# A hybrid two-layer backbone on one core: the RWKV stage, its group norms and the Hyena filters put in a recorded order, and late conditioning moved to VectorE

## The chip, the cores and the metric

The kernel runs on one core of a Trainium2 chip. A core has a matrix engine (TensorE, PE), three engines for element-wise work (VectorE or DVE, ScalarE or ACT, GpSimd or POOL) and SyncE (SP), which here issues every DMA. Each engine works through its own instructions in order; semaphores order the engines among each other. The metric is the device time of one execution in microseconds (us), lower is better.

## What is computed

Two layers over 1024 latent tokens of width 1024, with 256 context tokens in front. Each layer: `n = rmsnorm(h) * (1 + scale) + shift`, a token mixer with output `y`, then `h = h + gate * y`. Shift, scale and gate are `silu(c) @ ada_w[i] + ada_b[i]`, for the vector `c` of the latents and for `c_ctx` of the context; this is the conditioning. Layer 0 mixes with retention and RWKV-7 side by side, layer 1 with a Hyena long convolution (by FFT, with filters from a small network) and a neighbourhood attention. All is float32; large products are made of three matmuls of rounded high and low parts. RWKV, per head of 64 and in both directions, is a recurrence:

```
def step(s, inp):
    r_t, w_t, k_t, v_t, kk_t, a_t = inp
    sa = einsum('bhvk,bhk->bhv', s, -kk_t)
    s = s * w_t + sa * (kk_t * a_t) + v_t * k_t      # outer products
    return s, einsum('bhvk,bhk->bhv', s, r_t)
...
gn = (rw_y - mean) * rsqrt(var + eps) * rw_ln_w + rw_ln_b
rw_o = (gn + bonus) * silu(u_gate)
```

## The kernel before

Tokens lie in 10 blocks of 128. The program runs in stages.

- **Stage A** (`phase_a`): the first layer's shift and scale (`ada_quarter`), the norms, and the dense projections. `Dense.cols` and `Shift.tile` multiply all tokens with 512 weight columns at a time, 24 matmuls for a PSUM tile (`dnp`, `mmps`), four PSUM buffers; `wtiles` loads weights (`wraw`) and splits them on ACT (`whi`) and POOL (`wlo`). Retention runs among it.
- **Stage B** (`phase_b`): RWKV in 10 groups `g` of 128 tokens per direction `d`, a group as two steps `t` of 64 tokens; 16 matrices of 64x64 (8 heads, two steps) per group and direction. `stage1` calls `half` for each direction and pair of head pairs (40 half-groups in all): `lora` makes decay and rate, ACT, DVE and POOL make the operands `AR` and `BK`, PE turns `BK` into `BT` (`btp`). Then PE makes scores `sc`, which DVE masks into `Ga` and `Gr`. `lora` has one PSUM buffer, `sc` and `btp` share two (`b1`).
- `inverse` inverts the unit-triangular 64x64 matrices: it stores `Ga` to DRAM, loads its diagonal 32-blocks as `AL`, 128 lanes of them, solves 31 steps of two DVE operations (`tm`, `RR`, L956 and L958), stores and loads back into `TT`. `merge` fills the off-diagonal 32-block with three products of 32x32x32 (`t11p`, `xp`, `t21p`, L979).
- `recur` carries the state, 20 times in sequence: `rp` (L993 with the state, L996 with `Ga`), copy to `RH`, `up` with `TT`, copy to `UV`, `sp` (L1008), state update `S`, `SP`; results `Yg` by `rp` with `Gr` (L1016). `RwkvOut.block` applies group norm and gate to a block once both directions have it.
- In the same stage run the rest of the conditioning (`ada_gate`, `ada_cols`: blocks of 128 columns, weight-stationary on two columns of `c`, `adaps` L327, `adat` L293) and, after the last `stage1`, the Hyena filters (`hyena_kernels`).
- **Stage C and later**: output projection of layer 0 (`ops` on `chi`), layer 1's dense projections, attention, convolution, output. None of it is touched by the change, but that the filters' last matmuls run among the first `ops`.

In what order an engine takes its instructions is decided when the program is built: a scheduler of the language simulates the program and takes the ready instruction of highest priority. `Rwkv.step` gives the RWKV work a higher priority than the rest, and the generators `side` and `blocks` lay conditioning and group norms between the steps.

## Time and profile before

| what | us |
|---|---|
| three runs, median (lowest, highest) | 2404.95 (2404.92, 2412.53) |
| the profiled execution, its own time | 2408.1 |
| its span | 2406.3 |
| PE busy | 2206.3 (92%) |
| DVE, ACT, POOL busy | 1213.9, 930.2, 791.6 |

The profile is of one execution. Busy time of PE counts a matmul from its start to its modelled end, so matmuls that follow each other overlap in it. A float32 matmul is two passes, and so two records. The granted clock is the share of TensorE's full 2.4 GHz that it was given; its other level is half of that. In the row of tenths for 40 slices of the span, PE stands at 6 to 9, and its clock falls below 9 tenths in slices 12 to 21, which are the RWKV stage, and in slice 33.

### The profile page before, as it was taken

To read this page: it belongs to the slowest core of one execution; us is meant where nothing else is said; L and a number is where in the kernel's file an instruction comes from. 1 tells how busy PE (TensorE), PEld (TensorE's weight loads), DVE (VectorE), ACT (ScalarE), POOL (GpSimd) and SP (SyncE) were. 2 spreads that over 40 slices of the span, in tenths; PEclk is the share of its full clock that TensorE was granted. 3 is DMA by queue.
4 is the path that set the end of the run, shared out by engine and by line. 5 is a ranking of instruction groups with operands and counts; after the bars stand their busy time and mean duration, and the time that the engine had idled before them with its cause. 6 is when DMAs were issued, how large, how long until landed. Compare 5 with 4: busy or idle time off the path is not lost. (4 is left out here: it accounts for less than half of the span.)

```text
span 2406.3 us, 44212 instructions
## 1 busy us (share of the span) xinstructions
PE 2206.3 (92%) x16800; PEld 1854.7 (77%) x16800; DVE 1213.9 (50%) x3043; ACT 930.2 (39%) x1996; POOL 791.6 (33%) x1040
## 2 busy tenths in 40 slices
PE   7999999999989788898868899999979999989997
PEld 3778878777856677777766689889968888878987
DVE  6301222234347687777777756610036666634438
ACT  4321124445345354444335543321124444444432
POOL 2313625453556243333214534521111011010133
PEclk9999999999988787788889999999989999999999
DMA  7323333544276544455455443433276462175453
GB/s 245 95 78 106 116 115 123 155 126 136 91 211 180 119 124 126 108 134 138 101 145 170 151 160 107 148 115 109 75 184 162 130 169 93 53 242 156 132 161 123
DMA packets 398365, 325.66 MB, mean 135 GB/s; under 512 B 135038, under 2 KB 337928, under 8 KB 397898
## 3 DMA queue, kind: packets, MB, share of 16 engines
q1 hardware_dynamic: 398154, 322.85, 46.5%
q8 instruction: 133, 2.18, 0.4%
q14 instruction: 78, 0.64, 0.1%
HBM read 227.58 MB, written 95.17 MB: 134 GB/s over the span
## 5 line engine op out<-in xcount | busy, mean ns | idle before, releaser
L386 POOL TENSOR_TENSOR wlo<-wraw,whi 128x512 fp32r<-128x512 f32 (+1 forms) x60 | 81.6, 1380 | 354.7 <-ACT whi L385 303.0
L418 PE MATMUL dps<-n1hi,whi 128*128 128x512 f32 x448 | 187.5, 418 | 0.1
L418 PE MATMUL dps<-n1hi,wlo 128*128 128x512 f32 x448 | 177.4, 396 | 0.0
L418 PE MATMUL dps<-n1lo,whi 128*128 128x512 f32 x448 | 177.1, 395 | 0.0
L418 PE MATMUL dnp<-wlo,nhi 128*128 128x512 f32 x400 | 159.1, 399 | 2.9 <-POOL wlo L402 2.9
L418 PE MATMUL dnp<-whi,nlo 128*128 128x512 f32 x400 | 158.3, 397 | 0.0
L418 PE MATMUL dnp<-whi,nhi 128*128 128x512 f32 x400 | 153.3, 399 | 1.6 <-ACT whi L401 1.6
L402 POOL TENSOR_TENSOR wlo<-wraw,whi 128x512 fp32r<-128x512 f32 (+1 forms) x72 | 92.3, 1291 | 131.4 <-ACT whi L401 126.5
L418 PE MATMUL mmps<-nhi,whi 128*128 128x512 f32 (+1 forms) x336 | 123.4, 368 | 2.9 <-ACT vto L533 2.1
L327 PE MATMUL adaps<-aw,sc 128*2 128x128 f32 (+1 forms) x640 | 114.2, 335 | 11.6 <-DMA aw<-in_ada_w 9.6
L418 PE MATMUL mmps<-nlo,whi 128*128 128x512 f32 (+1 forms) x336 | 120.8, 361 | 0.0
L418 PE MATMUL mmps<-nhi,wlo 128*128 128x512 f32 (+1 forms) x336 | 119.6, 365 | 0.0
L956 DVE TENSOR_TENSOR tm<-RR,AL 128x126 f32<-128x126 f32 (+22 forms) x310 | 99.7, 322 | 19.5 <-DMA AL<-la 13.3
L1254 POOL TENSOR_TENSOR hn<-hn,xr 128x256 f32<-128x256 f32 x60 | 47.2, 791 | 175.4 <-DVE hn L1253 158.8
L418 PEld LDWEIGHTS dps<-n1hi,wlo 128*128 128x128 f32 x448 | 85.1, 190 | 18.6
L327 PEld LDWEIGHTS adaps<-aw,sc 128*2 128x2 f32 x640 | 55.3, 94 | 56.4 <-issue 16.7
L958 DVE TENSOR_TENSOR RR<-RR,tm 128x126 f32<-128x126 f32 (+22 forms) x310 | 94.6, 305 | 6.2
L418 PE MATMUL ops<-whi,clo 128*128 128x256 f32 x320 | 89.7, 287 | 6.1 <-DVE clo L1187 6.1
L418 PEld LDWEIGHTS dps<-n1hi,whi 128*128 128x128 f32 x448 | 85.9, 192 | 11.0 <-ACT whi L385 0.6
L418 PEld LDWEIGHTS dps<-n1lo,whi 128*128 128x128 f32 x448 | 85.6, 191 | 10.5
L418 PE MATMUL ops<-whi,chi 128*128 128x256 f32 x320 | 92.8, 292 | 0.0
L418 PEld LDWEIGHTS dnp<-wlo,nhi 128*128 128x128 f32 x400 | 75.7, 189 | 22.0 <-POOL wlo L402 4.7
(400 smaller groups left out, 6188.9 us busy)
## 6 DMA issues: line engine op xcount, KB each, us to landing
aw<-in_ada_w SPq DMA_DIRECT2D x32, 512.0 KB
kkr<-kkr SPq DMA_DIRECT2D x40, 384.0 KB
wraw<-in_odd_w_in SPq DMA_DIRECT2D x56, 256.0 KB
wraw<-in_even_w_in SPq DMA_DIRECT2D x48, 256.0 KB
bi<-in_nab SPq DMA_DIRECT2D x64, 192.0 KB
aw<-in_ada_w SPq DMA_DIRECT2D x8, 1024.0 KB
spec<-KS SPq DMA_DIRECT2D x32, 256.0 KB
h<-hn SPq DMA_DIRECT2D x16, 512.0 KB
```

Of the source, the lines that this page charges most:

```text
L327: nc.tensor.matmul(ps[0:2, :n], self.sc[:, k, :], w[:, k, :], start=k == 0, stop=k == 7)
L386: (lo_eng or nc.gpsimd).tensor_tensor(lo[:, kk:kk + 4], raw, hi[:, kk:kk + 4].bitcast(F32), op=ALU.subtract)
L402: nc.gpsimd.tensor_tensor(lo[:, :n], raw[:, :n], hi[:, :n].bitcast(F32), op=ALU.subtract)
L418: nc.tensor.matmul(ps, a, b, start=start and n == 0, stop=stop and n == 3 * nk - 1)
L956: nc.vector.tensor_tensor(t3, RR[:, 0:n, q:q + 1].to_broadcast([P, n, w]), AL[:, q:q + 1, q + 1:32].to_broadcast([P, n, w]), op=ALU.mult)
L958: nc.vector.tensor_tensor(RR[:, 0:n, q + 1:32], RR[:, 0:n, q + 1:32], t3, op=ALU.add)
L1254: add.tensor_tensor(h[:, cs], h[:, cs], x[:, cs], op=ALU.add)
```

## The change

What it does, in the order of the program:

- `ada_block`: the vector `c` is padded to 32 columns (`scw`), and the eight products of a block go to four column groups of 32; the four partial sums are added by the small matmul with `sel` that turns them.
- Conditioning that ran in stage B (both gates, layer 1's shift and scale) runs in stage A (`ada_late`): DVE adds up weight tiles of 128x512 times `c`, 16 operations a block of 512 columns, 8 blocks; PE sums over the partitions once a block. `Dense.cols` and `Shift.tile` advance it by one tile after each of their PSUM tiles.
- Stage B is written as generators which say what engine they need, for how long, and what they wait for; `Sched` plays them through when the program is built, with fixed durations, and the five engines keep that order.
- `lora` makes both directions at once, matmuls of the two row halves in turn; it takes two `b1` buffers, which it now shares with `sc` and `btp`.
- One eviction masks a whole `sc` tile into `G`, which replaces `Ga` and `Gr`.
- `inverse` works on 16-blocks: 15 steps of two operations, on POOL. `merge` makes the full inverse from the block-diagonal one by four rounds of 64x64x64 products (`mg`) with a DVE eviction after each; a round goes in two halves of eight matrices.
- In `recur` matmuls with a zero half use 64 rows instead of 128, and `sp` takes its two output halves in turn.
- Filters end within stage B's order; their operands have two buffers where they had one, and `psh` two PSUM buffers.

```
+class Sched:
+    HOP, LOOK = 0.12, 0.15
+    ...
+    def run(self):
+        while True:
+            ...
+            first = {}
+            for _, e, _, at, *_ in self.ready:
+                first[e] = min(first.get(e, 1e9), max(self.free.get(e, 0.0), at))
+            e = min(first, key=first.get)
+            r = min((r for r in self.ready if r[1] == e and r[3] <= first[e] + self.LOOK * (e != "")), key=lambda r: r[0])
+            ...
+    def ada_late(self, pool, psp):
+        ...
+        for layer, c0 in [(0, 2048 + 512 * j) for j in range(2)] + [(1, 512 * j) for j in range(6)]:
+            acc = [pool.tile([P, 512], F32, name="acc", tag=f"acc{j}", bufs=2) for j in range(2)]
+            for k in range(8):
+                w = pool.tile([P, 512], F32, name="aw", tag="aw", bufs=3)
+                nc.sync.dma_start(w, self.i["ada_w"][layer, k * P:(k + 1) * P, c0:c0 + 512])
+                for j in range(2):
+                    c = self.sc[:, k, j:j + 1]
+                    if k:
+                        nc.vector.scalar_tensor_tensor(acc[j], w, c, acc[j], op0=ALU.mult, op1=ALU.add)
+                    else:
+                        nc.vector.tensor_scalar(acc[j], w, c, None, op0=ALU.mult)
+                yield
...
         for k in range(8):
-            nc.tensor.matmul(ps[0:2, :n], self.sc[:, k, :], w[:, k, :], start=k == 0, stop=k == 7)
-        return ps[0:2, :n]
+            g = 32 * (k % 4)
+            nc.tensor.matmul(ps[g:g + 32, :n], self.sc[:, k, :], w[:, k, :], start=k < 4, stop=k > 3)
+        return ps[:, :n]
...
+    def lora(self, g, hp):
+        ...
+        pss = [self.b1([P, 2, 2, P], "lora") for _ in range(2)]
+        for j, w in enumerate((self.w2, self.a2)):
+            for q, d in itertools.product(range(2), range(2)):
+                p = 2 * hp + q
+                nc.tensor.matmul(pss[d][:, j, q, :], w[HALF[d], p * P:(p + 1) * P], wa[HALF[d], j, :], start=True, stop=True)
...
+    def inverse(self, g):
+        ...
+        yield "get", "al"
+        ...
+        nc.sync.dma_start(AL, self.blocks("la", g))
+        t += 4.5
+        for q in range(15):
+            t = yield "POOL", 0.63, t
+            ...
+            nc.gpsimd.tensor_tensor(t3, RR[:, 0:n, q:q + 1].to_broadcast([P, n, w]),
+                                    AL[:, q:q + 1, q + 1:16].to_broadcast([P, n, w]), op=ALU.mult)
+            nc.gpsimd.tensor_tensor(RR[:, 0:n, q + 1:16], RR[:, 0:n, q + 1:16], t3, op=ALU.add)
...
+    def merge(self, g):
+        ...
+        for j in range(4):
+            for hp in range(2):
+                ...
+                ps = self.pc.tile([P, 8, C], F32, name="mg", tag="mg", bufs=1)
+                for u in range(8):
+                    for d in range(2):
+                        ...
+                        nc.tensor.matmul(ps[HALF[d], u, :], lh, rh, start=True, stop=True)
...
-            for h, p, d in each:
-                nc.tensor.matmul(sp[HALF[h], p, d, :], R["bt"][d, p // 2][:, (p % 2) * NS + t, h * C:h * C + C], uh(d, t, p, h),
+            for p, d, h in itertools.product(range(4), range(2), range(2)):
+                nc.tensor.matmul(sp[HALF[h], p, d, :], half("bt", d, p)[:, (p % 2) * NS + t, h * C:h * C + C], uh(d, p, h),
                                  start=True, stop=True)
...
+        E = mybir.EngineType
+        with tc.manual_schedule(engines={E.PE, E.DVE, E.Activation, E.Pool, E.SP}):
+            sch.run()
```

How instructions stand at three places, before and after. On PE, where a group's inverse is completed among other groups' scores; before:

```order
L979 MATMUL xp<-TX,Ga 32x32 x32
L921 MATMUL sc<-AR,BK 128x128 x8
L857 MATMUL lora<-wa,a_6097 128x128 x2
L327 MATMUL adaps<-aw,sc 2x128 x8
L979 MATMUL t21p<-TT_6116,TY 32x32 x32
L891 MATMUL btp<-cst,BK 128x128 x4
```

At the same work after (`mg` is the PSUM tile of `merge`, `HTt` the off-diagonal factor):

```order
L1239 MATMUL mg<-lt,G 64x64 x16
L989 MATMUL lora<-wa,w_6448 128x128 x4
L989 MATMUL lora<-wa,a_6449 128x128 x4
L1239 MATMUL mg<-lt,G 64x64 x16
L1239 MATMUL mg<-ld,HTt 64x64 x16
L1120 MATMUL sc<-AR,BK 128x128 x4
L1239 MATMUL mg<-ld,HTt 64x64 x16
```

The conditioning (`adaps`) is gone from between them, and the merge stands in runs of 16 instead of 32.

On DVE in the RWKV stage, where a group's substitution runs; before:

```order
L958 TENSOR_TENSOR RR<-RR,tm 128x7x18
L865 SCALAR_TENSOR_TENSOR cum<-scm,tw 128x256
L981 COPY TX<-t11p 32x512
L923 TENSOR_TENSOR Ga<-sc,cst 128x256
L925 TENSOR_TENSOR Gr<-sc,cst 128x256
L956 TENSOR_TENSOR tm<-RR,AL 128x136
L290 COPY adarow<-adaps 2x128
```

After, the same engine with the recurrence's copies (`RH`, `UV`) and the merge's evictions (`HTt`):

```order
L1287 COPY RH<-rp_8719 64x512
L1122 TENSOR_TENSOR G<-sc,cst 128x2x2x128
L1298 COPY UV<-up 64x512
L1050 SCALAR_TENSOR_TENSOR AR<-kkr,Pt_6461 128x4x64
L1122 TENSOR_TENSOR G<-sc,cst 128x2x2x128
L1309 TENSOR_TENSOR S<-S,sp 128x512
L1311 TENSOR_TENSOR S<-S,PCt 128x512
L1038 SCALAR_TENSOR_TENSOR cum<-scm,tw 128x256
L1083 SCALAR_TENSOR_TENSOR tw<-tw,kkr 128x256
L1244 TENSOR_TENSOR HTt<-mg,cst 128x512
```

And POOL after, which had none of the substitution before; `km`, `AR`, `BK` and `PCt` are the operands of the next half-group:

```order
L1196 TENSOR_TENSOR tm<-RR,AL 128x28
L1198 TENSOR_TENSOR RR<-RR,tm 128x14x2
L1196 TENSOR_TENSOR tm<-RR,AL 128x15
L1198 TENSOR_TENSOR RR<-RR,tm 128x15
L1085 TENSOR_TENSOR km<-km,kkr 128x256
L1053 TENSOR_TENSOR AR<-kkr,Pt_6460 128x4x64
L1090 TENSOR_TENSOR BK<-tw,Pi 128x4x64
```

The substitution has moved from among DVE's evictions to a closed run on POOL, ahead of the operands of later groups.

On DVE in stage A, at the first gate and the first query and key block; before:

```order
L649 SCALAR_TENSOR_TENSOR gt<-th,dnp 128x512 x10
L615 TENSOR_TENSOR rqk<-dnp,rope 128x512
L616 TENSOR_TENSOR rb<-dnp,rope 128x512
L615 TENSOR_TENSOR rqk<-dnp,rope 128x512
L616 TENSOR_TENSOR rb<-dnp,rope 128x512
```

After, with the late conditioning's sums (`acc`) between the evictions of the dense tiles (`dnp`):

```order
L385 SCALAR_TENSOR_TENSOR acc<-aw,scw,acc 128x512 x14
L750 SCALAR_TENSOR_TENSOR gt<-th,dnp 128x512 x8
L387 TENSOR_SCALAR acc<-aw,scw 128x512
L396 TENSOR_TENSOR adab<-adaps,adab 2x512
L387 TENSOR_SCALAR acc<-aw,scw 128x512
L385 SCALAR_TENSOR_TENSOR acc<-aw,scw,acc 128x512 x7
L750 SCALAR_TENSOR_TENSOR gt<-th,dnp 128x512
L385 SCALAR_TENSOR_TENSOR acc<-aw,scw,acc 128x512 x7
```

The sums stand in runs of up to 14 in front of evictions.

## Rows read from the trace of the kernel before

**Rows 1.** Stretches: length; busy us (count) of PE, PEld, DVE, ACT, POOL; clock; DMA.

```profile
58.50:672.90 614.40, 595.76 (x3028) 469.26 (x3027) 161.56 (x320) 216.25 (x391) 270.72 (x394) 0.99 0.38 114
...
1200.00:1393.80 193.80, 156.53 (x1593) 127.03 (x1593) 142.18 (x326) 93.13 (x193) 77.87 (x87) 0.91 0.48 149
...
672.90:1434.00 761.10, 651.87 (x7502) 539.58 (x7501) 548.43 (x1434) 345.48 (x774) 302.53 (x436) 0.85 0.53 144
692.80:1195.50 502.70, 436.25 (x5479) 364.60 (x5478) 376.70 (x1046) 224.88 (x539) 204.06 (x333) 0.82 0.54 135
```

**Rows 2.** Tiles: passes, ns min/median/max of one, first and last start.

```profile
L418 PE MATMUL mmps<-nhi,wlo x336: 276/394/629, 381.3 to 672.9; 128*128 128x512 f32 x112, 128*128 128x256 f32 x56
...
L857 PE MATMUL lora<-wa,w x160: 272/273/581, 692.8 to 1144.6; 64*128 64x128 f32 x160
...
L921 PE MATMUL sc<-AR,BK x640: 271/272/580, 707.9 to 1195.5; 64*128 64x128 f32 x160
...
L418 PE MATMUL ops<-whi,chi x320: 274/281/682, 1393.8 to 1540.0; 128*128 128x256 f32 x160
```

**Rows 3.** PE groups, 672.9 to 1434: passes | busy us, mean ns | idle before, releaser.

```profile
L921 PE MATMUL sc<-AR,BK 64*128 64x128 f32 x640 | 87.0, 307 | 4.9 <-DVE Gr L925 3.9 <-DVE tm L956 0.8
L327 PE MATMUL adaps<-aw,sc 128*2 128x128 f32 x512 | 81.5, 316 | 2.5 <-DVE adarow L341 1.2 <-DVE mc L295 0.8 <-DMA aw<-in_ada_w 0.5
...
L1008 PE MATMUL sp<-UV,BT 128*64 128x64 f32 x640 | 43.6, 243 | 5.2 <-DVE UV L1005 5.1
...
L857 PE MATMUL lora<-wa,w 64*128 64x128 f32 x160 | 34.9, 348 | 1.2 <-ACT tw L861 1.0
L857 PE MATMUL lora<-wa,a 64*128 64x128 f32 x160 | 34.8, 348 | 11.6 <-ACT tw L861 11.6
...
L1388 PE MATMUL d2ps<-d2r,f 128*128 128x512 f32 x47 | 27.5, 668 | 2.6 <-ACT S L1368 1.1 <-ACT d2r L1381 1.1 <-ACT KS L1347 0.4
L996 PE MATMUL rp<-UV,Ga 128*64 128x64 f32 x640 | 25.8, 229 | 0.0
...
L979 PE MATMUL t21p<-TT,TY 32*32 32x32 f32 x640 | 16.3, 218 | 8.8 <-DVE TY L981 8.6
L979 PE MATMUL t11p<-cst,TT 128*32 128x32 f32 x640 | 15.8, 210 | 8.1 <-DMA TT<-lt 8.1
L979 PE MATMUL xp<-TX,Ga 32*32 32x32 f32 x640 | 15.6, 213 | 5.1 <-DVE TX L981 5.1
...
L293 PE MATMUL adat<-cst,adarow 2*128 2x2 f32 x32 | 7.1, 288 | 11.5 <-DVE adarow L290 11.5
...
L418 PE MATMUL mmps<-nlo,whi 128*128 128x256 f32 x1 | 0.3, 281 | 0.0
```

**Rows 4.** PE in order of time: start, us, instruction.

```profile
715.85 0.27 PE L857 MATMUL lora<-wa,a 64*128 64x128 f32 x1
715.86 0.27 PE L921 MATMUL sc<-AR,BK 64*128 64x128 f32 x1
715.96 0.27 PE L857 MATMUL lora<-wa,a 64*128 64x128 f32 x1
```

**Rows 5.** DVE groups, 672.9 to 1434, columns as in rows 3.

```profile
L956 DVE TENSOR_TENSOR tm<-RR,AL 128x126 f32<-128x126 f32 (+22 forms) x310 | 99.7, 322 | 19.5 <-DMA AL<-la 13.3
L958 DVE TENSOR_TENSOR RR<-RR,tm 128x126 f32<-128x126 f32 (+22 forms) x310 | 94.6, 305 | 6.2
...
L1327 DVE TENSOR_TENSOR HK<-hkps,win 128x512 f32<-128x512 f32 x32 | 22.0, 686 | 11.6 <-PE hkps L1325 6.7 <-POOL EO L1332 4.7
...
L1094 DVE TENSOR_TENSOR fa<-fa,fv 128x512 f32<-128x512 f32 x10 | 8.4, 841 | 3.3 <-POOL fa L1093 3.2
```

**Rows 6.** POOL groups around the RWKV stage, columns as in rows 3.

```profile
L888 POOL COPY PCt<-Pt 128x4 f32<-128x4 f32 x40 | 9.9, 259 | 5.7 <-ACT Pt L870 3.4 <-DVE S L1011 1.4 <-DVE tm L956 0.9
...
L734 POOL TENSOR_TENSOR st<-SS,gch 64x128 f32<-64x128 f32 x18 | 8.3, 458 | 1.3
```

**Rows 7.** PE in order of time, start of the program, one conditioning product.

```profile
50.97 3.61 PE L327 MATMUL adaps<-aw,sc 128*2 128x256 f32 x16
```

More of the change, by code (lines that the diff above doesn't have):

```diff
@@ new lines, in __init__, with start @@
+        self.T = {}
+    def start(self):
+        add, ALL = self.sch.add, range(self.NG)
+        for g in ALL:
+            add(2 + g / 100, self.wa(g))
+            for hp in range(2):
+                add(2 + g / 100 + hp / 1000, self.lora(g, hp))
+            for n in range(4 * g, 4 * g + 4):
+                r = 2 + g / 100 + n % 4 / 2000
+                for f in (self.load, self.chain, self.keys, self.scores, self.turn, self.end):
+                    add(r, f(n))
+            for t in range(self.NS):
+                add(1.5, self.values(g, t))
+            add(1 + g / 100, self.inverse(g))
+            add(0.5, self.merge(g))
+        add(0, self.recur())
@@ L862, in half, with chain @@
-        th, ta = tw[:, 0], tw[:, 1]
+        return [nat(L[:, :, j, :]) for j in range(3)], v4, u4
+    def chain(self, n):
+        nc, sch, T, pf, C = self.s.nc, self.sch, self.T, self.pf, self.C
+        g, d, hp = self.split(n)
+        ca, cr = (0, 64) if d == 0 else (64, 0)
+        yield "wait", ("tw", n), ("kkr", n)
+        yield "get", "tmp"
+        (kt, kkt, rt), v4, u4 = self.views(n)
+        th = T["tw", n][:, 0]
+        t = yield "ACT", 0.43
+        sch.mark(("tmp", n), t)
         nc.scalar.activation(th, th, AF.Copy, scale=0.5, bias=0.5)
-        cum = pf.tile([P, 2, P], F32, name="cum", tag="cum", bufs=1)
+        yield "DVE", 0.87
+        cum = pf.tile([P, 2, P], F32, name="cum", tag="cum", bufs=2)
@@ L983, in recur, with end @@
-    def recur(self, g, R):
-        s, D, pl, pc, C, NS = self.s, self.D, self.pl, self.pc, self.C, self.NS
-        nc, S, SP, RH = s.nc, self.S, self.SP, self.RH
-        uh = lambda d, t, p, h: R["uv"][d, t][:, p, h * C:h * C + C]
-        each = [(h, p, d) for h in range(2) for p in range(4) for d in range(2)]
-        copy = (nc.vector.tensor_copy, nc.scalar.copy)
-        for t in range(NS):
+        sch.put("b1", t)
+        sch.mark(("bt", n), t)
+    def end(self, n):
+        t = yield "wait", ("used", n), ("ar", n)
+        self.sch.put("kkr", t)
+        t = yield "wait", ("prod", n), ("G", n), ("bt", n), ("pc", n)
+        self.sch.put("tmp", t)
+        if n % 2:
+            yield "wait", ("used", n - 1)
+            self.sch.put("tw", t)
@@ L1013, in recur @@
             for h in range(2):
+                yield "ACT", 0.62
                 nc.scalar.copy(SP[HALF[h], :, :, h, :], S[HALF[h]])
[L1015 to L1024 removed]
@@ L1146, in phase_b, with after_scores, over @@
-    return hy, right, f1
-def phase_c(s, D, hy, right, keep):
+        sf = ExitStack()
+        pf, pb, ph = pool(sf, "b_f", side="right"), pool(sf, "b_ps", space=PSUM), pool(st, "b_h")
+        rw = Rwkv(s, D, sch, pl, pc, pf, pb)
+        f1 = []
+        def after_scores():
+            sf.close()
+            f1.append(pool(keep, "f1", side="right").tile([P, 8, 2, 2, 64], F32, name="f1"))
+            return f1[0], pool(right, "b_k", side="right"), pool(right, "b_kp", space=PSUM)
+        def over():
+            n = 4 * rw.NG - 4
+            t = yield ("wait", *((k, n + j) for j in range(4) for k in ("prod", "G", "bt", "pc")))
+            sch.mark("over", t)
@@ L1173, in phase_c @@
              for c in range(4)]
-        for _ in hy:
-            pass
         n1 = None
@@ L1207, in phase_c @@
             if not n1:
-                right.close()
                 pn = pool(keep, "n1", side="right")
```

987 lines of the change are left out of this document (640 added, 347 removed).

## The prediction

> **What bounds the kernel now.** I read the stretches first, then the first and last starts of the tiles that mark stages, then the TensorE (PE) groups of the middle stage, then single matmuls, then VectorE (DVE) and GpSimd (POOL).
>
> [rows 1] cut the span where its character changes. In the dense stage A (58.5 to 672.9 us) PE is busy 595.8 of 614.4 us, 97%, at a granted clock of 0.99: only less PE work helps there. In the middle, stage B, from the last dense matmul at 672.9 us to 1434.0 us, PE is busy 651.9 of 761.1 us, 86%, at a mean clock of 0.85, so part of it at 1.2 GHz; DVE is busy 548.4, ScalarE (ACT) 345.5, POOL 302.5. No engine is full. 110 of the core's idle PE microseconds lie here, and this is the stage that the change rewrites.
>
> [rows 2] give the marks: dense matmuls start until 672.9, `lora` opens stage B at 692.8, the last score matmul starts at 1195.5, the first output projection (`ops` on `chi`) at 1393.8. A few filter matmuls run among the projections until 1434, which is why I close the stage there; what follows is untouched, and I count it as before.
>
> **The change, part by part.** PE groups overlap at their edges: the 34 groups of the stretch, from 87.0 to 0.3 us [rows 3], sum to 754.3 us against a union of 651.9, so a group counts 0.864 of its own busy time.
>
> 1. Conditioning leaves stage B. `adaps` is 81.5 us and `adat` 7.1 us [rows 3], 88.6 together: 88.6 x 0.864 = 77 us less on PE.
>
> 2. `lora` alternates the two row halves. Now all passes of a `lora` use the same 64 rows, 34.9 + 34.8 us [rows 3]. Where a `lora` and an `sc` pass on different halves meet, two start within 0.01 us and the next 0.11 us later [rows 4], so two go at once. Half of 69.7 x 0.864 is 30 us less; if the pairs don't form, 0.
>
> 3. The state product `sp` alternates its output halves. It costs 43.6 us for 320 matmuls, 136 ns each; `rp` on `Ga`, of the same size but with halves alternating, 25.8 us, 81 ns each [rows 3]. 17.8 x 0.864 = 15 us less.
>
> 4. The inverse works on 16-blocks and is completed by 1280 matmuls of 64x64x64 instead of 960 of 32x32x32. The three old groups cost 16.3 + 15.8 + 15.6 = 47.7 us [rows 3]. No 64x64x64 pair exists in the trace. Nearest: the 81 ns above, 103 us in all, 55.5 x 0.864 = 48 us more. Low end: the 49 ns of an `xp` (15.6 / 320), 13 us more. High end: 136 ns, 109 us more. I take 48, since that row has the same columns and alternation.
>
> 5. DVE loses the 620 substitution steps, 99.7 + 94.6 = 194.3 us [rows 5]. It gains 80 merge evictions of 128x512, 0.686 us each as `HK` [rows 5], 55 us against 21 us for the old copies at the same price. The masks stay alike (80 evictions for 160 of half the size). All in all DVE comes to some 385 us.
>
> 6. POOL gains 300 steps of at most 64 elements. Between the 259 ns of a four-element copy and the 458 ns of a 64-element product [rows 6] they cost 78 to 137 us; with 107 and without the memsets of UV, POOL ends near 385 us. Half of these steps wait for the step before, and behind the stage's own POOL work: that latency is a rival below. ACT loses copies and stays near 335.
>
> 7. PE work left in the stretch: 651.9 - 77 - 30 - 15 + 48 = 578 us. It is still the fullest engine by far, so the time is this divided by how full PE can be kept. Two rows bound it: 86%, today's stage B, and 97%, the dense stage, which hardly waits. I take the middle, 91.3%: for more, because DVE goes from 72% of the stretch to about 60%, and its substitution steps no longer stand between an eviction and the matmul that waits for it; for no more, because the chain of the recurrence stays, and filling with conditioning in the first 100 us is gone. 578 / 0.913 = 633 us, 128 less than 761. If the order recorded in advance misjudges a wait, everything behind it on that engine waits too, SyncE's (SP) DMA issues included; 86% would still give 672, 89 less.
>
> 8. Stage A takes the conditioning. 128 DVE operations of 128x512, at most 0.841 us each as `fa` [rows 5], are 108 us, put on a DVE that is busy 161.6 of 614.4 us [rows 1]. They hide behind PE as long as evictions wait less than the four PSUM buffers allow. On PE come 8 matmuls of 512 columns, 1.15 us each by `d2ps` (27.5 us for the stretch's 24 [rows 3]), and 32 of one column, at most 7.1 / 16 = 0.44 each: 9 to 23 us, and stage A has no idle time to hide them. I take 12. The 64 loads of 256 KB move the same bytes as the 32 taken out of B; they pass SP ahead of weight loads in A, which have a spare buffer. At the start eight conditioning products of 3.6 us each [rows 7] are spread over four column groups; most of it waits for loads, so 5 us less (0 to 8). Together 7 us more.
>
> 9. The tail. The filters no longer mix with the output projections: their last two transforms run alone on PE, with evictions between. I count that within the 91.3%.
>
> Sum: -128 + 7 = -121 us on an execution of 2408.1 us (span 2406.3): 2287. The median of the runs shown, 2405.0, lies 3 us lower: **2284 us**.
>
> **A rule beside the rows.** Two of the old merge products, `xp` and `t21p`, alternate row groups within one PSUM bank, and `xp`, on 32 rows, costs 15.6 us where `t11p`, on all rows, costs 15.8 [rows 3]: no sign of a wait, though passes of 32 columns may be too short to show one. The Trainium skill, TensorEngine Tiling (Array Packing), Restrictions and Gotchas, says that different row tiles cannot access the same PSUM bank at the same time. By that rule the new merges, whose two row halves write one bank, would go one by one; the time is the second rival's.
>
> **The rivals.**
>
> *Denser than that.* With 49 ns merges (543 us of PE work) and PE at 97%, stage B takes 560 us: -201 + 7, 2211 us. For it: PE would be the only full engine, and a denser PE holds the higher clock, as 0.99 in stage A shows. Against it: [rows 1], where even the last part before the projections, mostly filters, keeps PE at 81%.
>
> *Merges one by one.* 136 ns each put 61 us more on PE: 639 / 0.913 = 700, -61 + 7, 2351 us. For it: `sp`, with its halves not alternating, shows that price. Against it: `xp`.
>
> *The freed time isn't used.* Work leaves PE and DVE, but the recurrence and the DMA round trips of the inverse set the pace, and PE idles instead. PE at 78% gives 741 us: -20 + 7, 2392 us. For it: 81% in the last stretch of [rows 1] at a DVE that is not full either. Against it: the substitution, the longest part of that round trip, halves its steps.
>
> *Slower: two PSUM buffers become the bound.* Before, `lora` has a buffer of its own beside the two of `sc` and `btp`; after, all three share two, and one `lora` takes both until ACT has read them. Per half-group that is four holds (two `sc`, one `btp`, one of `lora`) on two buffers. Today the 40 half-groups take 502.7 us [rows 1], 12.6 each, so it decides from 6.3 us a hold. A hold needs 1.09 us of matmuls (87.0 / 80) and 0.69 of eviction, 1.8 us; queued behind other work on DVE and ACT it could reach 7 us: 14 x 40 = 560, 57 more, +7: 2469 us. Against it: that needs over 4 us of queueing at every hold.
>
> **How the numbers follow.** Forecast 0.47 (its own range 2245 to 2325), denser 0.20, merges one by one 0.13, not used 0.13, slower 0.07. The range runs from 2200, below the densest case, to 2375, above the merge case and the better part of the unused one; left out are the rest of that case and the slower one, under 0.2. A difference of 0.3% (7 us) is about what a measurement of this kernel can tell from none. Forecast, denser, merges and most of the unused case lie more than that below 2405: faster 0.90; a little of the unused case: same 0.03; slower 0.07.
>
> **What would show it.** The last dense matmul starts 5 to 20 us later than 672.9 and `ops` on `chi` first near 1290. PE groups after: no `adaps` past the dense stage, `lora` near 35 us, `sp` near 26, the merges (`mg`) near 103; 62 or 174 would speak for the bounds. PE in stage B should be busy about 91% of some 630 us; below 80% the unused case is right. A dense stage longer by over 25 us would mean that the DVE bursts or the extra loads hold up its evictions. I would be wrong altogether if `lora` waits for buffers more than it does now, or if stage B is not shorter.

## The result and the profile after

The changed kernel takes 2379.6 us (median of four runs, 2369.9 to 2385.6) against 2408.7 us before (four runs, 2404.9 to 2420.4): a ratio of 0.988, 95% interval 0.9847 to 0.9913. The forecast was 2284 us, the range 2200 to 2375. The sign was right, a quarter of the gain came (29 us of 121), and the time lies 5 us outside the range. The profiled execution after took 2369.9 us, span 2368.1; it is the fastest of the four, and the account by stages below is of this one.

The same four cuts serve both kernels: the last dense matmul (`mmps`), the first and the last state product (`sp`), and the last matmul of the first output projection (`ops`). I call the stretch from the last dense matmul to the first `sp` the lead-in, and that from the first to the last `sp` the recurrence. Tiles of after (passes, ns of one, first and last start); those of before are [rows 2]:

```profile
L514 PE MATMUL mmps<-nhi,wlo x336: 276/393/632, 410.7 to 714.9; 128*128 128x512 f32 x112, 128*128 128x256 f32 x56
...
L989 PE MATMUL lora<-wa,w x160: 272/373/579, 760.4 to 1135.5; 64*128 64x128 f32 x160
...
L514 PE MATMUL ops<-whi,chi x320: 274/281/684, 1380.3 to 1511.7; 128*128 128x256 f32 x160
```

Stretches of before between these cuts, after its dense stage [rows 1] (length; busy us and count of PE, PEld, DVE, ACT, POOL; clock; DMA share; GB/s):

```profile
672.90:817.90 145.00, 128.71 (x1015) 93.98 (x1014) 97.74 (x250) 74.99 (x190) 73.19 (x113) 0.80 0.70 185
817.90:1294.50 476.60, 399.66 (x5748) 348.01 (x5747) 358.88 (x1005) 197.51 (x446) 159.80 (x251) 0.83 0.49 125
1294.50:1540.20 245.70, 223.66 (x1574) 195.66 (x1571) 160.85 (x361) 108.61 (x198) 115.90 (x106) 0.98 0.46 148
1540.20:2406.30 866.10, 812.48 (x5219) 724.92 (x5217) 399.01 (x1004) 308.21 (x731) 157.52 (x162) 0.98 0.47 137
```

The same of after, with the dense stage as the first row:

```profile
52.60:714.90 662.30, 630.45 (x3142) 487.08 (x3140) 274.89 (x467) 217.74 (x395) 284.00 (x396) 0.97 0.44 131
714.90:860.30 145.40, 96.09 (x763) 76.63 (x761) 51.53 (x92) 61.98 (x159) 74.65 (x141) 0.61 0.50 124
860.30:1254.90 394.60, 345.90 (x6068) 309.39 (x6070) 261.51 (x468) 193.21 (x455) 232.57 (x457) 0.94 0.65 146
1254.90:1512.00 257.10, 221.87 (x1580) 194.20 (x1576) 153.10 (x352) 106.36 (x196) 114.63 (x102) 0.98 0.43 138
1512.00:2368.10 856.10, 806.40 (x5219) 719.79 (x5217) 397.12 (x1004) 308.71 (x731) 157.55 (x162) 0.98 0.48 139
```

So the account is: start -6, dense stage +48, lead-in 0, recurrence -82, filters and first projection +11, the rest -10; together the 38 us between the two spans. Most of the gain is in the recurrence, and the dense stage gives more than half of it back. The rest has the same code in both kernels; in the runs below that stretch takes 855 to 866 us, so its 10 us are scatter.

TensorE groups of after from 714.9 to 1420 us (passes | busy us, mean ns | idle before, releaser), and the conditioning's two groups in the dense stage; [rows 3] are those of before, and one more of before stands last:

```profile
L1239 PE MATMUL mg<-TT,HTt 64*64 64x64 f32 x1280 | 49.2, 230 | 8.7 <-DVE TT L1248 8.7
L1239 PE MATMUL mg<-lt,G 64*64 64x64 f32 x640 | 27.0, 235 | 4.4 <-DMA lt<-lt 3.4 <-DVE HTt L1244 0.9
L1302 PE MATMUL sp<-UV,BT 128*64 128x64 f32 x640 | 25.5, 239 | 10.4 <-DVE UV L1298 10.4
L1239 PE MATMUL mg<-ld,HTt 64*64 64x64 f32 x640 | 23.8, 226 | 2.7 <-DVE HTt L1244 1.7 <-DVE TT L1248 1.0
L989 PE MATMUL lora<-wa,w 64*128 64x128 f32 x160 | 22.3, 366 | 21.1 <-DMA wa<-wa 16.3 <-ACT tw L998 2.4 <-DVE G L1122 2.4
L989 PE MATMUL lora<-wa,a 64*128 64x128 f32 x160 | 17.3, 320 | 0.0
...
L1120 PE MATMUL sc<-AR,BK 64*128 64x128 f32 x640 | 106.7, 320 | 22.0 <-POOL BK L1092 14.1 <-DVE G L1122 2.3 <-ACT BT L1146 2.0
...
L1324 PE MATMUL rp<-UV,G 128*64 128x64 f32 x640 | 23.6, 231 | 0.0
```

```profile
L395 PE MATMUL adaps<-acc,one 128*2 128x512 f32 x16 | 9.2, 704 | 0.5 <-ACT vto L633 0.5
L403 PE MATMUL adaps<-one,acc 128*128 128x1 f32 x64 | 7.9, 244 | 0.0
```

```profile
L1016 PE MATMUL rp<-UV,Gr 128*64 128x64 f32 x640 | 52.9, 246 | 3.6 <-ACT UV L1005 3.6
```

The prices of the parts that the forecast named are close to it: merges 100.0 us, `sp` 25.5, `lora` 39.6 as the sum of its two groups. (These two now overlap; together they keep TensorE busy 33.9 us, where the 69.7 us of before did not overlap.) What the parts were worth is not close.

### The profile page after: what moved, and what is told of

The parts are those of the page before. It is cut to its first block, busy times and chain, and to the rows that moved or that the text cites. A ratio compares the mean times of both kernels' runs of the same rounds, so it can differ in the third digit from the quotient of the medians.

```text
span 2368.1 us, 44174 instructions
## 1 busy us (share of the span) xinstructions
PE 2130.7 (90%) x16976; PEld 1807.1 (76%) x16976; DVE 1172.1 (49%) x2487; ACT 912.2 (39%) x1976; POOL 875.7 (37%) x1271
## 5 line engine op out<-in xcount | busy, mean ns | idle before, releaser
L514 PE MATMUL dnp<-whi,nhi 128*128 128x512 f32 x400 | 160.1, 411 | 1.4 <-ACT whi L497 1.3
L1120 PE MATMUL sc<-AR,BK 64*128 64x128 f32 x640 | 106.7, 320 | 22.0 <-POOL BK L1092 14.1
L514 PE MATMUL mmps<-nhi,wlo 128*128 128x512 f32 (+1 forms) x336 | 121.1, 368 | 0.1
L1120 PEld LDWEIGHTS sc<-AR,BK 64*128 64x128 f32 x640 | 90.6, 219 | 32.7 <-POOL BK L1092 15.1
L385 DVE SCALAR_TENSOR_TENSOR acc<-aw,scw,acc 128x512 f32<-128x512 f32 x112 | 96.8, 915 | 22.0 <-DMA aw<-in_ada_w 21.6
L497 ACT ACTIVATE whi<-wraw 128x512 fp32r<-128x512 f32 (+1 forms) x72 | 43.0, 605 | 135.7 <-DMA wraw<-in_even_w_in 91.6
L514 PEld LDWEIGHTS dnp<-whi,nhi 128*128 128x128 f32 x400 | 76.3, 192 | 21.4 <-ACT whi L497 4.0
```

The lines of the kernel that those rows point to most:

```text
L385: nc.vector.scalar_tensor_tensor(acc[j], w, c, acc[j], op0=ALU.mult, op1=ALU.add)
L497: nc.scalar.activation(hi[:, :n], raw[:, :n], AF.Copy)
L514: nc.tensor.matmul(ps, a, b, start=start and n == 0, stop=stop and n == 3 * nk - 1)
L1120: nc.tensor.matmul(ps[:, u, :], T["bk", n][HALF[h], u, :], T["ar", n][HALF[h], u, :], start=True, stop=True)
```

## The experiments

Each row is a profiled execution cut as above, with the median of the timed runs and their ratio to runs of before that were timed beside them (medians 2407 to 2411 us).

| kernel | dense stage | lead-in: to `lora` + on | recurrence | DVE busy in it | median us | ratio (95%) |
|---|---|---|---|---|---|---|
| before | 614.4 | 19.9 + 125.1 | 476.6 | 358.9 | 2408.7 | 1 |
| after | 662.3 | 45.5 + 99.9 | 394.6 | 261.5 | 2379.6 | 0.988 (0.9847-0.9913) |
| a1 | 640.6 | 54.5 + 100.4 | 400.5 | 261.4 | 2370.5 | 0.9836 (0.9816-0.9856) |
| a2 | 655.3 | 45.8 + 99.9 | 405.5 | 259.1 | 2375.5 | 0.9864 (0.984-0.9888) |
| a3 | 653.8 | 46.2 + 100.2 | 400.4 | 262.2 | 2376.6 | 0.9866 (0.9845-0.9887) |
| a4 | 615.2 | 54.4 + 110.8 | 451.5 | 327.9 | 2406.9 | 0.9985 (0.997-0.9999) |
| a5 | 662.4 | 18.2 + 121.1 | 423.7 | 264.5 | 2402.6 | 0.9971 (0.9953-0.999) |
| a6 | 646.8 | 16.8 + 99.8 | 401.5 | 261.7 | 2340.7 | 0.971 (0.967-0.975) |
| a7 | 614.9 | 54.4 + 113.6 | 410.0 | 271.6 | 2365.5 | 0.9801 (0.977-0.9831) |
| a8 | 636.2 | 16.8 + 114.1 | 418.8 | 271.7 | 2355.9 | 0.9793 (0.9755-0.9832) |
| a9 | 661.4 | 45.8 + 108.9 | 407.0 | 261.8 | 2393.8 | 0.9941 (0.9918-0.9965) |
| a10 | 662.6 | 46.5 + 99.7 | 402.5 | 261.3 | 2385.1 | 0.9921 (0.989-0.9952) |
| a11 | 666.1 | 46.0 + 121.8 | 503.0 | 258.2 | 2502.0 | 1.0409 (1.0367-1.0451) |
| b1 | 618.2 | 13.6 + 158.2 | 480.4 | 359.4 | 2436.1 | 1.0093 (1.0058-1.0129) |
| b2 | 617.9 | 13.8 + 129.7 | 481.9 | 359.4 | 2417.3 | 1.0035 (1.0016-1.0055) |
| c1 | 663.8 | 46.4 + 100.7 | 463.9 | 321.4 | 2443.7 | 1.0141 (1.0121-1.016) |
| c2 | 666.8 | 17.9 + 143.6 | 487.9 | 277.1 | 2457.7 | 1.0208 (1.0187-1.0229) |
| c3 | 638.5 | 21.0 + 114.0 | 447.2 | 279.3 | 2383.5 | 0.99 (0.9883-0.9918) |
| c4 | 637.7 | 22.8 + 115.3 | 415.3 | 270.4 | 2362.2 | 0.9804 (0.9772-0.9836) |
| c5 | 657.4 | 46.6 + 99.4 | 404.9 | 260.5 | 2384.5 | 0.9912 (0.9878-0.9947) |

Where the RWKV stage is the changed kernel's own (after, a1 to a3, a6), its recurrence reads 394.6 to 405.5 us: that is the scatter against which a difference in that column has to stand, and against before the gain is 71 to 82 us. Where the dense stage is the changed kernel's own (after, a5, a9 to a11, c1, c2, c5), it reads 657.4 to 666.8 us. The expectations count the recurrence and its first step from the first `rp`, which in after starts 6.5 us ahead of the first `sp` (853.8 against 860.3 us).

### What the conditioning costs the dense stage (a1 to a3)

a1 does the loads and VectorE steps for the first of eight row blocks only, a2 all loads, a3 all VectorE steps on one load:

```
 for k in range(8):
+    if k: yield; continue                     # a1
     w = pool.tile(...); nc.sync.dma_start(w, ...)   # a3: only if k == 0
     for j in range(2):                              # a2: multiply only if k == 0
```

> The changed kernel with only the first of the eight row blocks of each conditioning block loaded and multiplied (8 loads and 16 VectorE operations in place of 64 and 128; the conditioning matmuls stay, so the modulation values and gates are wrong). From the first dense matmul to the last the changed kernel takes 662 us against 614 before. Theory 'conditioning holds up the dense stage': most of the 48 us go with this, only the conditioning's own 17 us of TensorE stay, so about 632 us here and about 2350 us in all (ratio to before near 0.975). Rival 'the dense stage grew for another reason' (the retention's share of it, the lower clock at its start, buffers): the stretch stays above 650 us and the time above 2370.

> The changed kernel with all 64 conditioning loads, but only the first row block of each conditioning block multiplied on VectorE (16 operations in place of 128). If the loads, which pass SyncE ahead of weight loads, cost the dense stage its time, it stays near 662 us and the whole near 2378. If VectorE's operations do it, by standing in front of evictions and weight preparation, it comes down to about 632 us and 2350 in all, as with the first row block only.

> The changed kernel with all 128 conditioning operations on VectorE, but each conditioning block loads only its first row block and uses it eight times (8 loads in place of 64). If VectorE's operations themselves cost the dense stage its time: near 662 us there, 2378 in all. If it is the loads, or VectorE standing still until a load lands with evictions queued behind it (21.6 us of such waits in the trace of after): about 632 us and 2350.

Without the late conditioning the dense stage takes 614.9 us (a7). With its matmuls and an eighth of the rest it takes 640.6, with the other loads added 655.3, with the other VectorE steps added instead 653.8, with both 662.3. No single part is to blame: the matmuls with that eighth bring 26 us, the other loads alone 15, the other steps alone 13, both together 22. (a2 and a3 lie only 2 to 4 us below the scatter of the full stage.) Neither forecast of a2 and a3 came, 632 or 662, and a1 stayed 9 us above its 632 and 20 above its 2350.

By [rows 1] and the rows above, 35 of the 48 us are busy time of TensorE (630.5 against 595.8), 17 of them the conditioning's own matmuls, and 13 are waits (31.9 us against 18.6). The other 18 us of busy time come with a granted clock of 0.97 in place of 0.99; no run takes them apart. The longest waits of after's dense stage (waited for: us, times, longest):

```profile
PE hyps L1791 <- DMA hw<-in_hw: 6.9, 1, 6.9
PE gtp L758 <- DVE gt L750: 6.5, 2, 3.3
PE dnp L514 <- POOL wlo L498: 4.3, 7, 1.4
```

The first, for a load of the filter network's weights, is not among before's waits of this stage; the others are there in smaller size.

The whole gained less than the stage in each case: in a1 the stage is 21.7 us shorter and the first `sp` comes 12 us sooner, because `lora` then starts 54.5 us behind the dense stage and not 45.5. Something else held it, which a5 and a6 ask.

### What holds the RWKV stage back (a5, a6)

SyncE's queue in after, between the last dense matmul and the first `lora` (start, us, line, transfer):

```profile
741.45 0.33 SPq L879 DMA_DIRECT2D cat<-rn  x1
741.83 0.43 SPq L872 DMA_DIRECT2D rG<-rz  x1
749.35 0.32 SPq L879 DMA_DIRECT2D cat<-rn  x1
749.71 0.43 SPq L929 DMA_DIRECT2D eye<-in_eyel  x1
750.19 1.76 SPq L1167 DMA_DIRECT2D UV<-vt  x3
752.06 1.00 SPq L935 DMA_DIRECT2D ld<-Z  x2
753.10 2.10 SPq L935 DMA_DIRECT2D lt<-Z  x2
755.24 1.27 SPq L1167 DMA_DIRECT2D UV<-vt  x1
756.56 1.34 SPq L970 DMA_DIRECT2D wa<-wa  x1
```

The retention of the dense stage still works for 30 us behind the last dense matmul; its last store waits until 749.35 us, and every load of the RWKV stage stands behind that store. In the order recorded in advance nothing of the stage comes ahead of what was left of the stage before, on any of the five engines. a5 takes SyncE out of the recorded order; a6 takes away the retention's fourth pair:

```
-with tc.manual_schedule(engines={E.PE, E.DVE, E.Activation, E.Pool, E.SP}):
+with tc.manual_schedule(engines={E.PE, E.DVE, E.Activation, E.Pool}):    # a5
-rt.pair(2 * g + p)
+if 2 * g + p < 3: rt.pair(2 * g + p)                                     # a6
```

> The changed kernel with SyncE's order in the RWKV stage left to the scheduler that orders the rest of the kernel; the other four engines keep the list scheduler's order. It puts the first loads of wa and kkr ahead of the retention's last stores, behind which they wait now. Theory 'head of line': lora's first matmul, at 760.4 us in after and 45 us behind the last dense matmul, then waits only for the retention's last matmul on TensorE and starts 12 to 14 us earlier; the whole about 2366 us, if SyncE's later order is no worse. Rival: the retention's own end sets the start and SyncE is not in the way: lora stays 45 us behind the last dense matmul and the time at 2379 or above.

> The changed kernel without the fourth of the retention's four head pairs (a copy of another array is stored in place of its result, so the output is wrong); it takes some 27 us of TensorE work out of the dense stage. Theory 'the retention's tail holds the RWKV stage back': with it gone lora starts some 20 us after the last dense matmul, as in before, not 45; both together some 50 us less, about 2330 us. Rival: the start hangs on the round trip of wa through memory or on the loads ahead of it on SyncE: lora stays 40 us or more behind the last dense matmul, and only the 27 us go, 2353 us.

In a5 `lora` starts 27 us sooner, twice what was forecast, and still the first `sp` comes only 6 us sooner and the whole takes 2402.6 us in place of the forecast 2366: the other scheduler's order of the loads lengthens the chain from `lora` on from 99.9 to 121.1 us, and the recurrence to 423.7. In a6 `lora` starts 16.8 us behind the dense stage and the chain keeps its 99.8, so the lead-in falls by 29 us. So of after's 45.5 us up to `lora` the retention's remainder, with the loads queued behind its store, holds 29; behind it come 100 us of chain, where before had 19.9 and 125.1. The chain is 25 us shorter than before's (without the list order, in c2, it takes 143.6), and the seam took the same amount back. The whole of a6, 2340.7 us, lies between its two forecasts, 2330 and 2353, and lacks the pair's work in the dense stage too (646.8 us).

### Where the conditioning may lie (a4, a7, a8, c3, c4)

a4 gives the conditioning, as VectorE steps, to the list scheduler of the RWKV stage; a7 does it there on TensorE in four column groups:

```
-side = s.ada_late(pool(st, "a_ada"), psp)
+s.ada_tasks(sch, pool(sf, "b_ada", side="right"), psh)   # rank 4.9: below all RWKV work
+# a4: 64 loads of 256 KB, 128 steps  acc = w * c + acc  on VectorE
+# a7: 16 loads of 1 MB, 128 matmuls  ps[32*(k%4):+32, :256] += sc[k].T @ w[k]
```

> The changed kernel with its conditioning (the same loads, VectorE operations and matmuls) taken out of the dense stage and given to the list scheduler of the RWKV stage at a low rank. In the changed kernel VectorE is busy only 48 of the first 139 us after the last dense matmul. Theory 'fill': that idle time takes most of the 110 us of VectorE work at little cost, the dense stage falls from 662 to about 617 us, and the whole comes to about 2340 us (ratio near 0.972). Rival 'the RWKV stage pays for it as the dense stage did': the RWKV stage grows by 30 us or more and the whole stays near 2375.

> The changed kernel with the conditioning of the RWKV stage done on TensorE as in before, but in four column groups at once (16 blocks of 256 columns, two VectorE operations each), given to the list scheduler at a low rank. Theory 'VectorE sets the recurrence's pace and TensorE has room at the start': the dense stage falls to about 615 us as without conditioning, the 139 us to the first recurrence step grow little, the recurrence keeps its 402 us (it took 462 with the conditioning on VectorE), and the whole comes to about 2345 us. Rival: whatever is added to this stage is paid for in full, by the transfers or the order: 2375 or above.

Both dense stages are at 615 us again. In a4 the recurrence grows by 57 us, for 66 us more of VectorE work in it; in a7 by 15, little more than the scatter. So the conditioning costs most on VectorE, in the recurrence (57 us) as in the dense stage (48), and least on TensorE in the RWKV stage. The lead-in of a7 is longer than after's by 23 us: the shorter dense stage leaves more of the retention behind it (54.4 us to `lora`), and the chain, 14 us longer, has the conditioning and its 1 MB loads beside it; which of these lengthens it was not tested.

a8 adds to a7 four buffers for each of the retention's loads, the `rz` matmuls behind the first q/k block, and a high priority for the retention; c4 leaves the priority out; c3 is a8 with the conditioning at rank 1.2, ahead of the key chains.

```
-qk = wk.tile([P, 12, 64], F32, name="qk", tag="qk", bufs=2)
+qk = wk.tile([P, 12, 64], F32, name="qk", tag="qk", bufs=4)   # and rk
-dn.gate("rz", 1536, True)
 for g in range(2):
     dn.qk(g)
+    if g == 0: dn.gate("rz", 1536, True)
     for p in range(2):
+        with s.tc.high_priority(offset=1000000):               # not in c4
             rt.pair(2 * g + p)
```

> The kernel of a7 (conditioning on TensorE in the RWKV stage) with the retention brought forward in the dense stage: its pairs get a high priority with the scheduler that orders that stage, four buffers for each of its two loads in place of two (room that the conditioning left), and the gate matmuls stand behind the first of the two q/k blocks. In a7 lora starts 54.6 us behind the last dense matmul and the first recurrence step 161.5 us behind it; without the retention's fourth pair (a6) 17 and 110. Theory 'the retention's tail sets the start of the RWKV stage': lora some 18 us and the first step 115 to 130 us behind the last dense matmul, the dense stage still about 615 us, and the whole near 2328 us. Rival: retention matmuls placed early wait on TensorE with dense ones queued behind them; the dense stage grows by 25 us or more and the whole stays at 2355 or above.

> The kernel of a8 without the high priority of the retention: four buffers for each of its loads and its earlier place in the dense stage stay. In a8 the dense stage grew from 615 to 636 us with the retention's matmuls in it, and the first recurrence step came 124.5 us behind it. Theory 'buffers and place are enough': dense stage at most 625 us, lora at most 25 us behind it, first step 10 us sooner than in a8's 813 us, the whole near 2345 us. Rival: what the dense stage gains the tail gives back; first step at 813 us or later and the whole at 2355 or above.

> The kernel of a8 with the conditioning at a rank ahead of the key chains, so that it is done before the recurrence or early in it. In a8 the first recurrence step came 124 us behind the last dense matmul and the recurrence took 426 us against 402 in the changed kernel. Theory 'conditioning in the recurrence is what costs there': recurrence 400 to 410 us, first step at most 8 us later, the whole near 2345. Rival: its loads stand in front of the chain's on SyncE, the first step comes 15 us or more later and the whole is at 2355 or above.

In a8 `lora` follows 16.8 us behind the dense stage, as forecast; the dense stage takes the retention's matmuls in (636.2 us), and the first `sp` comes at 820.0 us in place of a7's 835.9. c4 is no better. In time all five are slower than forecast: a4, a7, a8, c4 and c3 were forecast at 2340, 2345, 2328, 2345 and 2345 us, and all but a7 are as slow as their rival said or slower. In c3 the recurrence takes 447 us although the conditioning's last product starts at 846 us; I did not find out why, and only note that a higher rank for work off the chain cost 28 us. a8 beats both kernels: 2355.9 us, 0.9793 of before.

### What the recurrence follows (b1, b2, c1, c2)

b1 takes the conditioning out of the RWKV stage of before; b2 has all its matmuls and steps again, on one load. c1 puts the inverse of after back on VectorE; c2 drops the recorded order:

```
-side = itertools.chain(s.ada_gate(0, ...), s.ada_cols(1, ...), s.ada_gate(1, ...))
+side = iter(())                                          # b1: constants instead
-nc.gpsimd.tensor_tensor(t3, RR[...], AL[...], op=ALU.mult)
+nc.vector.tensor_tensor(t3, RR[...], AL[...], op=ALU.mult)   # c1, and the step after it
-with tc.manual_schedule(engines={...}): sch.run()
+sch.run()                                                # c2
```

> The kernel before without the conditioning that runs in its RWKV stage (gates and modulation values are constants, so wrong). The prediction's first term took 88.6 us of conditioning matmuls times 0.864 = 77 us off the stage: about 2330 us, ratio 0.968. Theory 'fill': of the conditioning matmuls 39 us lie in the first 128 us after the last dense matmul, where the chain from lora to the first recurrence step sets the pace, and cost nothing there; only the 49 us behind them count: 2365 us or more, ratio 0.982 or more, and the first recurrence step does not come earlier.

> The kernel before with all conditioning matmuls and VectorE steps of its RWKV stage, but one load in place of 32, used by all of them (gates and modulation values wrong). Without any conditioning (b1) the kernel took 2436 us against 2411. Theory 'filling': the matmuls keep TensorE going and its clock up while the recurrence waits; with them back the time is that of before, 2400 to 2412 us. Rival 'the order that the scheduler chose by chance, or the loads as pacemaker, made b1 slow': with the loads gone it stays near 2436.

> The changed kernel with the 300 steps of the inverse on VectorE in place of GpSimd, all else alike. Theory 'VectorE sets the recurrence's pace': its 110 us of conditioning cost the recurrence 60 us in a4, so some 60 to 70 us of steps cost 30 to 40, and the whole is 2410 to 2420 us. Rival 'GpSimd's slower steps lie on the path': the first recurrence step comes sooner and the whole is at or below 2380.

> The changed kernel with its RWKV stage left to the scheduler that orders the rest of the kernel, on all five engines. Theory 'the list scheduler's order made the gain': the recurrence goes back towards its 477 us, the whole to 2430 or above, though lora may start 25 us sooner. Rival 'the work taken from VectorE and TensorE made it': the recurrence keeps about 400 us and the whole is at or below 2385.

The recurrence of each (columns as above), b1, b2, c1 and c2 in turn:

```profile
852.00:1332.40 480.40, 375.66 (x5428) 341.67 (x5428) 359.39 (x966) 193.66 (x442) 160.02 (x249) 0.76 0.42 106
```

```profile
824.20:1306.10 481.90, 402.88 (x5737) 353.86 (x5737) 359.37 (x1000) 196.00 (x443) 159.53 (x252) 0.82 0.41 105
```

```profile
863.90:1327.80 463.90, 388.99 (x6112) 347.66 (x6114) 321.37 (x722) 199.09 (x474) 165.49 (x223) 0.85 0.56 127
```

```profile
880.90:1368.80 487.90, 412.58 (x6176) 369.55 (x6174) 277.11 (x519) 202.85 (x482) 240.12 (x473) 0.87 0.53 123
```

b1 has 309 passes fewer in the recurrence than b2, and the recurrence takes the same time: TensorE is idle more, and at a lower clock (0.76 against 0.82) its other matmuls, as many in both, take 376 us against 359. In the lead-in the absence even costs 28 us (171.8 against 143.5), and the whole is 2436 us, where b2, forecast at 2400 to 2412, takes 2417. Taking this filling away was worth nothing here.

c1 and c2 show what the 82 us hang on. With the inverse on VectorE (60 us more there) the recurrence takes 464 us, twice the increase that was forecast; without the list order 488, though VectorE has only 277 us to do. Each alone undoes the gain or most of it, so their shares do not add up. c1 also changes the order that is recorded, and the 16-blocks of the inverse, the single mask and the 64-row matmuls were not undone one by one. With the list order, the recurrence is longer in the two kernels with most VectorE work: 261.5 us of it go with 395, 271.6 with 410, 321.4 with 464, 327.9 with 452 (after, a7, c1, a4). It is not the only thing: c3, with 279.3, takes 447.

TensorE's busy time is no measure of work here: c1 and after issue nearly the same matmuls in this stretch (6112 and 6068 passes) and have 389.0 and 345.9 us of it, at clocks of 0.85 and 0.94. Of the 69 us by which c1's recurrence is longer, 43 are this busy time and 26 are waits (74.9 us against 48.7).

### TensorE's own terms (a9, a10, a11, c5)

```
+nc.tensor.matmul(ps[:, 0:256], s.ident, s.cst[:, 0:256], ...)   # a9: 71 times, lowest rank, until the first merge
-for q, d in itertools.product(range(2), range(2)):
+for d, q in itertools.product(range(2), range(2)):               # a10, lora
-for u in range(8):
-    for d in range(2):
+for d in range(2):
+    for u in range(8):                                           # a11, merge
-for p, d, h in itertools.product(range(4), range(2), range(2)):
+for h, p, d in each:                                             # c5, sp
```

> The changed kernel with some 70 matmuls of 128x128x256 on constants, which nobody reads, given to the list scheduler at the lowest rank from the first lora to the end of the first merge; nothing else is changed. In the 93 us from the first lora to the first recurrence step TensorE's granted clock is 0.57 in after. Theory 'clock': the filler lifts it to 0.9 or more, the chain's own matmuls take half the time, the first step comes 10 to 20 us sooner and the whole is 2362 to 2372 us. Rival 'the chain is made of evictions, GpSimd steps and transfers': the clock rises, but the first step comes no sooner, or later where a filler stands in front of the chain; 2378 us or more.

> The changed kernel with lora's matmuls in the order of before, all of one row half and then all of the other. The prediction gave the alternation 30 us of TensorE work. If so, lora's busy time goes from 39.6 us back to 66 us or more, and the time up by at most 25 us, less where the stage waits for something else. If the order of the halves does nothing: 40 us and the same time.

> The changed kernel with each merge's 16 matmuls of 64x64x64 in the order of halves (eight of one, then eight of the other) in place of alternating. The merges' busy time is 100 us in after. If alternating row halves of one PSUM bank run side by side, it goes to about 136 ns each, 174 us, and the whole becomes 30 to 65 us longer, near 2425; if they are done one by one in any case, busy time and total stay.

> The changed kernel with the state product sp in the order of before (eight matmuls of one output half, then eight of the other). The prediction gave the alternation 15 us. sp's busy time goes from 25.5 us to about 43; if TensorE's work bounds the recurrence, the whole becomes 12 to 18 us longer, near 2395; since sp stands on the path from one step to the next, 20 x 0.9 us would also come through a pure chain. If the halves' order does nothing: 26 us and 2380.

a9 raises the clock in the lead-in, from 0.61 to 0.78, and the chain from `lora` on gets 9 us longer, as the rival had it. The lead-in of a9, then of a6:

```profile
713.80:868.70 154.90, 119.66 (x905) 92.00 (x903) 51.80 (x92) 62.42 (x159) 74.74 (x141) 0.78 0.48 119
```

```profile
699.20:816.00 116.80, 74.58 (x661) 64.12 (x659) 43.65 (x70) 44.53 (x131) 71.43 (x138) 0.61 0.52 128
```

With the recorded order, then, raising the clock by filler did not pay: the low clock of the lead-in looks like a sign of waiting more than its cause. That is not shown to the end, since fillers also stand in front of the chain's own matmuls and may hide a gain. In before the filler did help (b1, b2); there the other scheduler also chose another order each time, and the two cannot be told apart from these runs.

The merges of a11, then `sp` of c5 (columns as in the groups above):

```profile
L1239 PE MATMUL mg<-TT,HTt 64*64 64x64 f32 x1280 | 107.3, 273 | 7.8 <-DVE TT L1248 7.8
L1239 PE MATMUL mg<-ld,HTt 64*64 64x64 f32 x640 | 45.6, 246 | 3.4 <-DVE HTt L1244 3.4
L1239 PE MATMUL mg<-lt,G 64*64 64x64 f32 x640 | 44.7, 240 | 3.1 <-DMA lt<-lt 3.1
```

```profile
L1302 PE MATMUL sp<-UV,BT 128*64 128x64 f32 x640 | 40.7, 234 | 10.4 <-DVE UV L1298 10.4
```

Alternating halves nearly double the rate of the merges: 100.0 us for 1280 matmuls, 78 ns each, against 197.6, 154 ns each. Those 98 us lengthen the recurrence by 108, the lead-in by 22 and the whole by 122, twice to four times the forecast. For `sp` the order is worth 15.2 us of busy time, as forecast, but the recurrence of c5, 404.9 us, lies within the scatter, and the whole, 2384.5 us, 10 below its forecast.

a10 says less than it was meant to. Its edit does not bring back the order of before, where one `lora` has passes of one row half alone: with both directions in one `lora`, two matmuls of one half stand in front of two of the other. One `lora` of before, after and a10 (start, us; `x` counts passes):

```profile
879.10 0.71 PE L857 MATMUL lora<-wa,w 64*128 64x128 f32 x4
```

```profile
934.29 0.71 PE L989 MATMUL lora<-wa,w 64*128 64x128 f32 x8
```

```profile
936.79 0.72 PE L989 MATMUL lora<-wa,w 64*128 64x128 f32 x8
```

In a10 too eight passes take the time of before's four, so the halves still run side by side. All passes of `lora` keep TensorE busy 69.7 us in before, 33.9 in after and 37.5 in a10 (46.2 against 39.6 as sums of groups). What the alternation is worth to the stage's time a10 therefore does not test. As for the recurrence, TensorE is busy 88% of it in after, 89% in c5 and 91% in a11: 15 us more fit between its waits, 98 do not.

## Why the prediction was wrong, step by step

- **Step 1, conditioning out of the stage, 77 us less: failed.** The matmuls went, as said, but they had been filling. Taking them out of before alone made it slower (b1) and left its recurrence as it was.
- **Steps 2 and 3, `lora` and `sp`:** right in size (33.9 us busy, 39.6 as groups, and 25.5 for 35 and 26). `lora` halved, from 69.7 us, as the pairs said. In time `sp`'s part was worth next to nothing (c5); for `lora` no run shows it.
- **Step 4, merges:** right, 100 us for 103. The Trainium skill, TensorEngine Tiling (Array Packing), Restrictions and Gotchas, says that different row tiles cannot access one PSUM bank at the same time. Here they do so at 78 ns a matmul against 154 with the halves apart; the measurement decides, and the rival "merges one by one" is out. The two halves of a merge write different partitions of the bank; for outputs in the same partitions no run shows anything.
- **Steps 5 and 6, VectorE and GpSimd:** the sums came out (397.6 and 375.9 us from 714.9 to 1406 us, the stretch that answers to 672.9 to 1434 of before; 385 each had been forecast). But I let them count only as a reason for a denser TensorE. VectorE's share of it and the order are what the recurrence's gain hangs on (c1, c2).
- **Step 7, 578 us of TensorE work at one share of 91.3%: the step that failed most.** From 714.9 to 1406 us (both stretches end 106 us before the end of the first projection) TensorE is busy 564.4 of 691.1 us, 82%. The work came out near 578, in part by luck: the sum had no term for `rp` on `Gr`, which fell from 52.9 to 23.6 us, nor for `sc`, which rose from 87.0 to 106.7. One share for the stage was wrong. It is 66% in the lead-in, 88% in the recurrence, 86% from there to the last projection. The stage gained 70 us in place of 128, and that is 58 of the 83 us by which the profiled execution misses the forecast gain of 121. That filling was gone in the first 100 us I had named, and priced at nothing; that the retention still ran there, with the new stage's loads queued behind its store, I had not seen at all, and a6 puts 29 us on it.
- **Step 8, the dense stage: failed in size.** 48 us longer in place of 12; the conditioning's matmuls took the 17 us that the bounds allowed, but loads and VectorE steps, each costed at nothing because others would hide them, brought most of the rest (22 us in a1 against after). The 6 us at the start came as forecast.
- **Step 9, the tail,** cost 11 us that I had put inside the 91%. The unchanged rest, 10 us shorter, lies within the scatter.
- **The rivals.** "The freed time isn't used" came nearest, 2392 us with a chance of 0.13: its idle TensorE is there, but in the lead-in and not in the recurrence, where PE is denser than before. Of "denser" only the clock came, and only in the recurrence (0.94 for 0.83); TensorE is 88% busy there, not 97%, and a merge costs 78 ns, not 49. The slower case, two PSUM buffers, does not show: `lora` waits 2.4 us for `G` and 2.4 for `tw`, less than the 11.6 before [rows 3]. What TensorE does wait for is `BK`, which GpSimd makes: 14.1 us in front of `sc`, which in before waited 4.9 us in all and not for it. The prediction named GpSimd's latency, but gave it no price of its own.

## What to carry to other kernels

Price work that is taken away by who waits for it, not by busy time: in a recurrence where neither engine was full, taking the conditioning from TensorE was worth nothing (b1), and 60 us of steps given back to VectorE cost 69 (c1). Give each stretch its own limit before a share of busy time is applied to it, and look at the seam where a recorded order begins, since all that the stage before still has open stands ahead of it on every queue. A stage at 97% hides no new work: an eighth of the loads and steps with their matmuls cost it 26 us, all of them 48.

## What the runs showed of the hardware that I had not expected

Matmuls on different row halves that write one PSUM bank, each half its own partitions, ran side by side (78 against 154 ns for 64x64x64 in float32). And TensorE's busy time for much the same matmuls was 345.9 us at a granted clock of 0.94 and 389.0 at 0.85, so that a stretch with more waits (74.9 us against 48.7) shows more TensorE work as well.
